# A bidirectional encoder trunk on one core: five seven-product pairs per feed-forward unit instead of three, with the residual added by transfers

## The chip, the cores and the metric

One Trainium2 chip, one of its cores. The metric is the device time of one execution in microseconds. The core has five engines, each of which takes its instructions in program order: PE (matrix multiply), DVE (elementwise, "VectorE"), ACT (activation functions, copies and casts, "ScalarE"), POOL (a general engine, "GpSimd") and SP, which here only starts transfers. Engines wait for one another by semaphores.

## The reference

A sequence of 256 tokens with 2048 features passes two layers. Each layer is `x = x + mixer(rmsnorm(x))`, then `x = x + swiglu(rmsnorm(x))`. The mixer of the first layer is grouped-query attention, that of the second a recurrent block. The change is in the feed-forward half of both layers:

```python
D_MODEL, SEQ, D_FF = 2048, 256, 5632

def rms_norm(x, g):
    y = x * lax.rsqrt(jnp.mean(x * x, axis=-1, keepdims=True) + EPS)
    return y * g

def swiglu(h, w_gate, w_up, w_down):
    return (jax.nn.silu(h @ w_gate) * (h @ w_up)) @ w_down

for i in range(DEPTH):              # DEPTH = 2
    h = rms_norm(x, norm_mix[i])
    ...                             # mixer
    x = x + swiglu(rms_norm(x, norm_ffn[i]), ffn_w_gate[i], ffn_w_up[i], ffn_w_down[i])
```

All data are float32.

## The kernel before

**Numbers in two parts.** PE multiplies in a reduced format. So each float32 operand is split into hi (the value cast, by ACT) and lo (the rest, value minus hi, by DVE), and a product of a 128 x 128 block of x with 512 columns of a weight is three matmuls: x hi by w hi, x lo by w hi, x hi by w lo (`product`, L294, L295, L297). Every weight passes once through the chain: a transfer into a `raw` tile, ACT's cast to `hi`, DVE's subtraction to `lo`, PE. There are five `raw` tiles, and in the feed-forward stage seven hi and seven lo tiles, used in turn; a tile is written again when its last reader is done.

**Units.** The 5632 hidden columns are 44 tiles of 128, taken four at a time in a *unit*: 11 units per layer, numbered 0 to 10. A unit computes 512 columns of gate and of up for all 256 tokens. It runs over eight *pairs* c0 to c7 of 128-row blocks of the 2048 rows. A plain pair is two `wide` calls, each with its own weight tile (1024 wide) and four products, eight products in all, into the banks c11 and c21, then c12 and c22. A *seven-product pair* uses Strassen's scheme in Winograd's form: seven products, from sums of the weight blocks made by DVE and sums of the x blocks made once per layer (`Norm.form`). Its products, in order, go to m1 (weight b11), c11 (b21), c12 (b22), p5 (t1), p7 (t3), p6 (t2) and c21 (t4). Its weights take three 1024-wide hi and lo tiles, called here A (b11 and b21), B (t1 and t3) and C (t2 and t4), and a half one, `ohi` and `olo` (b22). `load_seven` makes them: A's split, the sums t1 and t3, the split of b22, the sums t2 and t4, then the splits of B and C.

Behind the last seven-product pair of a unit ACT copies m1 out of its bank (L734), and DVE combines it with p6, p5 and p7 (L735 to L738). When c7 is done, DVE adds c11 and c21 (L741), ACT applies silu, DVE forms the hidden values (L744, L745) and transposes them in blocks of 32 (L377); 16 copies on ACT, the *turn* (L384), put the blocks in place, and ACT and DVE split the result (L747, L748).

**Down groups.** The units of a layer fall into five parts of 2, 2, 2, 2 and 3. From unit 3 on, each unit is preceded by two of the four groups that multiply the part before by its rows of w_down: a group is 512 output columns, 16 products for these parts, into two banks of the same pool as m1, p5, p7 and p6 (four banks, in turn). DVE adds a group's banks to the residual x (`add_residual`, L318). The last part's groups stand at the end of the layer and also feed the next norm.

**Order.** PE's order is that of the code; a scheduler sets that of the other engines when the program is built. `follow` ties casts to casts and rests to rests, so that weights are prepared in the order of use.

Tiles with the same tag share `bufs` buffers: a new one waits until the old one's readers are done.

Of the kernel before, what the change touches and what calls it, by code (L numbers as in the profile page):

```python
# [15 lines left out]
ALU = mybir.AluOpType  # L16
AX = mybir.AxisListType

P = 128
S = 256  # L20
D = 2048
KT = D // P
# [4 lines left out]
DFF = 5632  # L27
PARTS = [8, 8, 8, 8, 12]
UNIT = 4
SEVEN = (0, 3, 5)  # L30
FEWER = (0, 5)
FEW = (1, 2)
HALF = 8
CHUNK = HALF * P
WIDE = 512
RING = 5
MORE = 2
NW = D // WIDE
COMMON = {"nsq", "ssq", "nm", "nr", "rsq_s"}
EPS = 1e-6  # L40
LRU_C = 8.0
GRID_W = 64
# [31 lines left out]
def trunk(ctx, tc, w, out):  # L74
# [32 lines left out]
    ring, held, ft = [0], [], []  # L107
# [80 lines left out]
    def ffn_order(l):  # L188
        seq = []
        for what, i in ffn_plan():  # L190
            if what == "down":
                seq += pairs(w[f"w_down{l}_{i[0]}"][i[1]])
                continue
            both = [(w[f"w_gate{l}"][i, c], w[f"w_up{l}"][i, c]) for c in range(KT // 2)]
            seq += sum(([b] if c in (FEWER if i in FEW else SEVEN) else list(b) for c, b in enumerate(both)), [])
        return seq + out_order(w[f"w_down{l}_{len(PARTS) - 1}"], UNIT // 2)

    order = [w["w_k"][i] for i in range(2 * KT // 4)]
# [50 lines left out]
    def new_acc():  # L249
        return ps_a.tile([P, 2 * S], F32, tag="acc", name=nm("acc"))  # L250
# [41 lines left out]
    def product(o, x, wt, start, stop):  # L292
        (xh, xl), (wh, wl) = x, wt
        pe.matmul(o, xh, wh, start=start, stop=False)  # L294
        pe.matmul(o, xl, wh, start=False, stop=False)  # L295
        step()
        pe.matmul(o, xh, wl, start=False, stop=stop)  # L297
        step()

    def wide(accs, xs, k0, total, fresh=None):  # L300
        hi, lo = half()
        fresh = fresh or (k0 == 0, k0 == 0)
        for j in range(CHUNK // WIDE):
            k = k0 + j
            wh, wl = (t[:, j * WIDE : (j + 1) * WIDE] for t in (hi, lo))
            for a in range(2):
                product(accs[a], block(xs, k, a), (wh, wl), j == 0 and fresh[a], k == total - 1)

    def wide_project(xs, total, bank=new_acc):
# [62 lines left out]


    def turn_blocks(src, engines, own=None):
        turned = tmp("turned", (P, 2, WIDE), bufs=1)
        own = tmp("hid", (P, 2, WIDE), bufs=1) if own is None else own
        dve.transpose(turned, src)  # L377
        t = own.rearrange("p a (b c) -> p (a b) c", c=S)
        for i in range(4):
            of = turned[32 * i : 32 * i + 32].rearrange("p a (k j c) -> p k a j c", k=4, j=4)  # L380
            for j in range(4):
                to = t[32 * j : 32 * j + 32].rearrange("p k (a i c) -> p k a i c", a=2, i=4)
                eng = engines[(4 * i + j) % len(engines)]
                (eng.copy if eng is act else eng.tensor_copy)(to[:, :, :, i, :], of[:, :, :, j, :])  # L384
        return t

    class Norm:
# [14 lines left out]
            self.xs.append(t)  # L402

        def square(self, g, a):
            sq = tmp("nsq", (P, WIDE), bufs=1)
            o = x_tm[:, a, g * WIDE : (g + 1) * WIDE]
            return act.activation(sq, o, AF.Square, accum_out=self.ss[:, a, g : g + 1])

# [15 lines left out]
                    self.form(2 * g + i, t[:, 2 * i : 2 * i + 2, :])  # L424

        def form(self, c, src):
            v, t = (tmp(f"e{i}", (P, 2 * S), bufs=1).rearrange("p (a b) -> p a b", a=n) for i, n in ((0, 2), (1, 4)))
            for j in range(2):
                act.activation(v[:, j, :], src[:, j, :], AF.Copy, scale=col(self.g[0], self.g[1] + 2 * c + j))
            (a11, a21), (a12, a22) = ([v[:, j, a * P : (a + 1) * P] for a in range(2)] for j in range(2))  # L430
            for i, x, y, op in (
                (0, a21, a22, ALU.subtract), (1, a11, a21, ALU.subtract),
                (2, t[:, 0, :], a11, ALU.subtract), (3, a12, t[:, 2, :], ALU.add),
            ):
                pool.tensor_tensor(t[:, i, :], x, y, op)
# [275 lines left out]
    def ffn(norm, nxt):  # L711
        def bank():
            return ps_m.tile([P, 2 * S], F32, tag="pm", name=nm("pm"))

        def unit(seven):
            xs, r = norm.xs, [norm.r[:, a : a + 1] for a in range(2)]
            m1, p5, p7, p6 = (bank() for _ in range(4))
            c11, c21, c12, c22 = (new_acc() for _ in range(4))
            for c in range(KT // 2):
                if c not in seven:  # L720
                    wide((c11, c21), xs, 2 * c, KT, (False, False))
                    wide((c12, c22), xs, 2 * c, KT, (False, c == 1))
                    continue
                wt, first, end = half(), c == seven[0], c == seven[-1]
                n1, n3, n2, n4 = norm.forms[c]
                a11, a12, a22 = block(xs, 2 * c, 0), block(xs, 2 * c + 1, 0), block(xs, 2 * c + 1, 1)
                for o, x, y in (
                    (m1, a11, "b11"), (c11, a12, "b21"), (c12, n4, "b22"), (p5, n1, "t1"),
                    (p7, n3, "t3"), (p6, n2, "t2"), (c21, a22, "t4"),
                ):  # L730
                    product(o, x, wt[y], first, end and any(o is m for m in (m1, p5, p7, p6)))
                if end:
                    base, v, u, x = (tmp(f"e{i}", (P, 2 * S), bufs=1) for i in range(4))
                    act.copy(base, m1)  # L734
                    dve.tensor_tensor(u, base, p6, ALU.add)  # L735
# [3 lines left out]
            h = tmp("hid", (P, 2, 2 * S), bufs=1)  # L739
            for o, y, b in ((base, base, c11), (u, u, c21)):  # L740
                dve.tensor_tensor(o, y, b, ALU.add)  # L741
            for a, (o, y, b) in enumerate(((base, v, c12), (u, x, c22))):
                table_act(o, o, AF.Silu, scale=r[a])
                dve.tensor_tensor(h[:, a, :], b, y, ALU.subtract)  # L744
                dve.scalar_tensor_tensor(h[:, a, :], h[:, a, :], r[a], o, ALU.mult, ALU.mult)  # L745
            t, ht = act_four(), turn_blocks(h, (act,), h)
            act.copy(t[:, :, :S], ht)  # L747
            dve.tensor_tensor(t[:, :, S:], ht, t[:, :, :S].bitcast(F32), ALU.subtract)  # L748
            return [t[:, k, :] for k in range(UNIT)]

        hid = [[] for _ in PARTS]
        ends = np.cumsum(PARTS) // UNIT
        for what, i in ffn_plan():
            if what == "unit":
                hid[int(np.searchsorted(ends, i, "right"))] += unit(FEWER if i in FEW else SEVEN)
            else:
                add_residual(i[1], wide_project(hid[i[0]], PARTS[i[0]], bank), None)
        if nxt is not None:
            ln_exp_tables()
        groups(hid[-1], PARTS[-1], PARTS[-1] - UNIT, lambda: None, partial(add_residual, norm=nxt, store=nxt is None))  # L760
        scope.pop()
        ft.pop().close()
# [216 lines left out]
```

## Time and profile before

| | |
|---|---|
| median of three runs | 2001.21 us (2000.93 to 2001.96) |
| the profiled execution | 2001.05 us, span 1999.3 us |
| busy: PE, DVE, ACT, POOL | 99%, 82%, 65%, 13% of the span |
| granted PE clock | 0.999 |
| three loads that carry the FFN weights | 176 each, 512 KB, 3.6 to 4.4 us to landing |

A page gives busy time by engine, and by source line the groups of instructions with their idle time before them and what ended it. A timeline row reads: start in us, duration in us, engine, line, operation, output and inputs with partitions x elements, count, and in brackets the idle time before it with its releaser. A row of a waits view reads: waiting engine, line and tile, then the one waited for, total us, times, longest. A row of a stretch gives its length, then busy us and instruction count for PE, PE's weight loads, DVE, ACT and POOL, then the clock, the share of transfer engines busy and GB/s. Instructions of an engine overlap a little at their ends, so what a run of them costs is read from start to start.

### The profile page before, as it was taken

Reading aid. Unit: us, or ns where it says so; the run is one execution under the profiler, and the core shown is the slowest. Engines: PE = TensorE matmul, PEld = TensorE weight load, DVE = VectorE, ACT = ScalarE, POOL = GpSimd, SP = SyncE. Lnnn points to the kernel's source line nnn. Section 1 sums busy time; section 2 is a strip of 40 time slices with the busy share of each in tenths; the row PEclk is TensorE's granted clock in tenths of the full one; section 3 lists DMA queues with packets and bytes.
Section 4 is the critical chain, followed back from the end, with each engine's and each line's share of the span. In section 5 each row is a group of like instructions: output and inputs, shape, how many; then the busy total and the mean of one; then the engine's idle time right before and its main releaser. Section 6 shows DMA issues by size and latency. Waiting matters only on the chain.

```text
span 1999.3 us, 27804 instructions
## 1 busy us (share of the span) xinstructions
PE 1981.1 (99%) x9940; PEld 1686.6 (84%) x9940; DVE 1629.9 (82%) x2154; ACT 1297.6 (65%) x1995; POOL 256.4 (13%) x315
## 2 busy tenths in 40 slices
PE   9999999999999999999999999999999999999999
PEld 8888888888888888888899998878888888888887
DVE  7989688888788887886779886897878887888873
ACT  7556577666656666567688887867655666556662
POOL 0443140000000000000455450410000000000000
PEclk9999999999999999999999999999999999999999
DMA  8543646656565565656556555566566555655664
GB/s 308 164 127 127 201 153 210 226 189 191 189 232 193 187 200 199 223 189 199 193 180 196 178 170 185 175 208 202 185 215 213 187 192 187 231 200 181 198 206 132
DMA packets 108570, 386.05 MB, mean 193 GB/s; under 512 B 12176, under 2 KB 12432, under 8 KB 108304
## 3 DMA queue, kind: packets, MB, share of 16 engines
q1 hardware_dynamic: 108288, 384.26, 58.3%
q8 instruction: 78, 1.28, 0.3%
q14 instruction: 60, 0.49, 0.1%
q10 hardware_dynamic: 144, 0.02, 0.0%
HBM read 382.13 MB, written 2.10 MB: 192 GB/s over the span
## 4 chain that ended last, share of the span: by engine, by line
PE 87%; DVE 7%; POOL 2%; issue 1%; ACT 1%; DMA 1%; SPq 0%; DVEq 0%; ACTq 0%; POOLq 0%
PE acc L294 16%; PE acc L295 16%; PE acc L297 16%; PE pm L297 8%; PE pm L295 8%; PE pm L294 8%; PE acc L274 3%; PE acc L275 3%; PE acc L276 3%; DVE lo L129 2%; PE acc L263 1%; POOL hb L548 1%; PE pm L275 1%; PE pm L276 1%; PE pm L274 1%
## 5 line engine op out<-in xcount | busy, mean ns | idle before, releaser
L129 DVE TENSOR_TENSOR lo<-raw,hi 128x1024 fp32r<-128x1024 f32 (+1 forms) x581 | 712.0, 1242 | 170.2 <-ACT hi L128 167.0
L128 ACT CAST hi<-raw 128x1024 fp32r<-128x1024 f32 (+1 forms) x581 | 596.6, 1048 | 299.1 <-PE acc L295 227.5
L294 PE MATMUL acc<-hi,xg 128*128 128x512 f32 x1036 | 403.3, 389 | 1.8 <-DVE e L741 1.4
L297 PE MATMUL acc<-lo,xg 128*128 128x512 f32 x1036 | 403.0, 389 | 0.0
L295 PE MATMUL acc<-hi,xg 128*128 128x512 f32 x1036 | 403.0, 389 | 0.0
L146 ACT CAST hi<-ws 128x1024 fp32r<-128x1024 f32 x124 | 130.6, 1054 | 194.5 <-DVE ws L152 192.3
L294 PEld LDWEIGHTS acc<-hi,xg 128*128 128x128 f32 x1036 | 194.5, 188 | 43.2 <-DVE e L741 2.3
L297 PEld LDWEIGHTS acc<-lo,xg 128*128 128x128 f32 x1036 | 194.5, 188 | 40.3
L295 PEld LDWEIGHTS acc<-hi,xg 128*128 128x128 f32 x1036 | 194.5, 188 | 40.3
L294 PE MATMUL pm<-hi,act 128*128 128x512 f32 x512 | 199.2, 389 | 0.0
L295 PE MATMUL pm<-hi,act 128*128 128x512 f32 x512 | 199.2, 389 | 0.0
L297 PE MATMUL pm<-lo,act 128*128 128x512 f32 x512 | 199.2, 389 | 0.0
L384 ACT COPY hid<-turned 32x256 f32<-32x256 f32 x436 | 175.9, 404 | 23.9 <-DVE turned L377 14.7
L294 PE MATMUL acc<-hi,act 128*128 128x512 f32 x448 | 174.6, 390 | 0.0
L297 PE MATMUL acc<-lo,act 128*128 128x512 f32 x448 | 174.4, 389 | 0.0
L295 PE MATMUL acc<-hi,act 128*128 128x512 f32 x448 | 174.3, 389 | 0.0
L149 DVE TENSOR_TENSOR lo<-ws,hi 128x1024 fp32r<-128x1024 f32 x124 | 151.8, 1225 | 6.4 <-ACT hi L146 3.6
L384 POOL COPY hid<-turned 32x256 f32<-32x256 f32 x84 | 52.3, 623 | 797.5 <-DVE turned L377 706.1
L274 PE MATMUL acc<-xg,hi 128*128 128x256 f32 x512 | 144.8, 283 | 0.0
L275 PE MATMUL acc<-xg,hi 128*128 128x256 f32 x512 | 144.6, 282 | 0.0
L276 PE MATMUL acc<-xg,lo 128*128 128x256 f32 x512 | 144.4, 282 | 0.0
L263 PE MATMUL acc<-xg,hi 128*128 128x512 f32 x384 | 126.6, 401 | 1.9 <-DVE xg L399 1.9
(215 smaller groups left out, 3435.7 us busy)
## 6 DMA issues: line engine op xcount, KB each, us to landing
raw<-in_w_gate_dram SPq DMA_DIRECT2D x176, 512.0 KB, 4.3
raw<-in_w_up_dram SPq DMA_DIRECT2D x176, 512.0 KB, 3.6
raw<-in_w_down_dram SPq DMA_DIRECT2D x176, 512.0 KB, 4.4
raw<-in_w_in_dram SPq DMA_DIRECT2D x64, 512.0 KB, 4.4
raw<-in_w_qv_dram SPq DMA_DIRECT2D x40, 512.0 KB, 3.9
raw<-in_w_o_dram SPq DMA_DIRECT2D x32, 512.0 KB, 3.6
raw<-in_w_out_dram SPq DMA_DIRECT2D x32, 512.0 KB, 4.0
graw<-in_w_gates_dram SPq DMA_DIRECT2D x32, 256.0 KB, 4.1
```

Of the source, the lines that this page charges most:

```text
L128: behind("cast", act.copy(hi[:, sl], raw[:, sl]))
L129: behind("rest", dve.tensor_tensor(lo[:, sl], raw[:, sl], hi[:, sl].bitcast(F32), ALU.subtract))
L146: behind("cast", act.copy(hi, src))
L149: return lambda: behind("rest", dve.tensor_tensor(lo, src, hi[:].bitcast(F32), ALU.subtract))
L263: pe.matmul(acc, w, xs[k], start=(k == 0), stop=stop)
L274: pe.matmul(o, hi, x[:, :S], start=start, stop=False)
L275: pe.matmul(o, hi, x[:, S:], start=False, stop=False)
L276: pe.matmul(o, lo, x[:, :S], start=False, stop=stop)
L294: pe.matmul(o, xh, wh, start=start, stop=False)
L295: pe.matmul(o, xl, wh, start=False, stop=False)
L297: pe.matmul(o, xh, wl, start=False, stop=stop)
L384: (eng.copy if eng is act else eng.tensor_copy)(to[:, :, :, i, :], of[:, :, :, j, :])
```

## The change

Units 3 to 10 of both layers take seven-product pairs at c0, c1, c3, c4 and c5 in place of c0, c3 and c5. Unit 0 keeps c0, c3 and c5; units 1 and 2 have c1 and c5 in place of c0 and c5. Which matmul starts a bank is no longer fixed to the first pair but found by `fresh`.

A unit's scratch is two tiles, `one` (base and u, later the transposed blocks) and `two` (v and x, then the hidden values), in place of six. The norm's forms and squares share a two-buffer tag `form`.

The groups of the first four parts no longer end in DVE's add: ACT copies each bank into a `form` tile, and a transfer that POOL issues adds the tile to x.

```diff
-SEVEN = (0, 3, 5)
-FEWER = (0, 5)
-FEW = (1, 2)
+SEVEN = (0, 1, 3, 4, 5)
+FEWER = {0: (0, 3, 5), 1: (1, 5), 2: (1, 5)}
...
         def form(self, c, src):
-            v, t = (tmp(f"e{i}", (P, 2 * S), bufs=1).rearrange("p (a b) -> p a b", a=n) for i, n in ((0, 2), (1, 4)))
+            v, t = (tmp("form", (P, 2 * S)).rearrange("p (a b) -> p a b", a=n) for n in (2, 4))
...
+            def fresh(o):
+                n = len(new)
+                new[:] = [b for b in new if b is not o]
+                return len(new) < n
...
                 if end:
-                    base, v, u, x = (tmp(f"e{i}", (P, 2 * S), bufs=1) for i in range(4))
+                    one, h = (tmp(n, (P, 2, WIDE), bufs=1) for n in ("one", "two"))
+                    (base, u), (v, x) = ([t[:, a, :] for a in range(2)] for t in (one, h))
                     act.copy(base, m1)
...
             else:
-                add_residual(i[1], wide_project(hid[i[0]], PARTS[i[0]], bank), None)
+                for a, acc in enumerate(wide_project(hid[i[0]], PARTS[i[0]], bank)):
+                    t = tmp("form", (P, WIDE))
+                    act.copy(t, acc)
+                    pool.dma_start(out=x_tm[:, a, i[1] * WIDE : (i[1] + 1) * WIDE], in_=t, accum_op=ALU.add)
```

What the scheduler makes of it on ACT is shown at two places. Lines after the change are one lower than before up to `form`, and some seven higher from the unit on (L734 becomes L741).

The first place is c5 of a unit in the steady part of a layer. Before, ACT has A, the half tile, B and C of c5 (L146), then four plain casts (L128), then the copy of m1 (L734):

```order
L146 CAST hi_1528_7286<-raw_1524_7280 128x1024
L146 CAST ohi_1530_7292<-raw_1525_7281 128x512
L146 CAST hi_1532_7296<-ws_1526_7284 128x1024
L146 CAST hi_1534_7301<-ws_1527_7285 128x1024
L128 CAST hi_1541_7337<-raw_1540_7336 128x1024
L128 CAST hi_1544_7355<-raw_1543_7354 128x1024
L128 CAST hi_1547_7373<-raw_1546_7372 128x1024
L128 CAST hi_1550_7391<-raw_1549_7390 128x1024
L734 COPY e0_1536_7327<-pm_1474_7070 128x512
```

Now the copy is L741 and the casts of seven-product weights are L145, and at the same place stands:

```order
L145 CAST hi_1242_5825<-raw_1238_5819 128x1024
L145 CAST ohi_1244_5831<-raw_1239_5820 128x512
L741 COPY one_1250_5866<-pm_1176_5587 128x512
L145 CAST hi_1246_5835<-ws_1240_5823 128x1024
L145 CAST hi_1248_5840<-ws_1241_5824 128x1024
L127 CAST hi_1253_5874<-raw_1252_5873 128x1024
```

The copy of m1 has moved from four casts behind c5's last to ahead of c5's B and C (`hi<-ws`). It stands so in units 4 to 10 of both layers; in unit 3 it stands between B and C.

The second place is where a unit's epilogue meets the next unit's first pair. On ACT before, the turn (L384) and then all of c0's casts:

```order
L128 CAST hi_1581_7571<-raw_1580_7570 128x1024
L384 COPY hid_1552_7408<-turned_1554_7418 32x8x32 x16
L146 CAST hi_1595_7604<-raw_1591_7598 128x1024
L146 CAST ohi_1597_7610<-raw_1592_7599 128x512
L747 CAST act_1553_7417<-hid_1552_7408 128x4x256
L146 CAST hi_1599_7614<-ws_1593_7602 128x1024
L146 CAST hi_1601_7619<-ws_1594_7603 128x1024
```

Now the turn is L383, the split's cast L753 and the copies of a group's two banks L765:

```order
L145 CAST hi_1188_5601<-raw_1184_5595 128x1024
L145 CAST ohi_1190_5607<-raw_1185_5596 128x512
L765 COPY form_1158_5501<-pm_1144_5427 128x512
L765 COPY form_1159_5504<-pm_1145_5428 128x512
L145 CAST hi_1192_5611<-ws_1186_5599 128x1024
L383 COPY two_1129_5320<-one_1143_5407 32x8x32 x16
L145 CAST hi_1194_5616<-ws_1187_5600 128x1024
L145 CAST hi_1200_5648<-raw_1196_5642 128x1024
L145 CAST ohi_1202_5654<-raw_1197_5643 128x512
L753 CAST act_1142_5406<-two_1129_5320 128x4x256
L765 COPY form_1174_5581<-pm_1160_5507 128x512
L765 COPY form_1175_5584<-pm_1161_5508 128x512
```

The turn has moved from ahead of c0's A to between c0's B and C, behind the two copies of the first group's banks; the second group's copies stand ahead of c1's B and C. It is so in units 4 to 10 of both layers.

The third place is DVE's own order there. Before, the transpose (L377), a plain rest, the two residual adds of the first group, and only then c0 of the next unit:

```order
L377 STREAM_TRANSPOSE turned_1009_4818<-hid_1007_4808 128x1024
L129 TENSOR_TENSOR lo_1037_4972<-raw_1035_4970,hi_1036_4971 128x1024
L318 TENSOR_TENSOR x_75<-x_75,pm_1010_4838 128x512
L318 TENSOR_TENSOR x_75<-x_75,pm_1011_4839 128x512
L149 TENSOR_TENSOR lo_1051_5005<-raw_1046_4998,hi_1050_5004 128x1024
```

Now:

```order
L148 TENSOR_TENSOR olo_1191_5608<-raw_1185_5596,ohi_1190_5607 128x512
L376 STREAM_TRANSPOSE one_1143_5407<-two_1129_5320 128x1024
L151 TENSOR_TENSOR ws_1187_5600<-ws_1186_5599,raw_1185_5596 128x512
L151 TENSOR_TENSOR ws_1187_5600<-ws_1187_5600,raw_1184_5595 128x512
L148 TENSOR_TENSOR lo_1193_5612<-ws_1186_5599,hi_1192_5611 128x1024
L148 TENSOR_TENSOR lo_1195_5617<-ws_1187_5600,hi_1194_5616 128x1024
```

The transpose has moved into c0's work, ahead of t2 and t4, and the adds to x are gone.

More of the change, by code (lines that the diff above doesn't have):

```diff
@@ L38 @@
 NW = D // WIDE
-COMMON = {"nsq", "ssq", "nm", "nr", "rsq_s"}
+COMMON = {"ssq", "nm", "nr", "rsq_s"}
 EPS = 1e-6
@@ L194, in ffn_order @@
             both = [(w[f"w_gate{l}"][i, c], w[f"w_up{l}"][i, c]) for c in range(KT // 2)]
-            seq += sum(([b] if c in (FEWER if i in FEW else SEVEN) else list(b) for c, b in enumerate(both)), [])
+            seq += sum(([b] if c in (FEWER.get(i, SEVEN)) else list(b) for c, b in enumerate(both)), [])
         return seq + out_order(w[f"w_down{l}_{len(PARTS) - 1}"], UNIT // 2)
@@ L374, in turn_blocks @@
     def turn_blocks(src, engines, own=None):
-        turned = tmp("turned", (P, 2, WIDE), bufs=1)
-        own = tmp("hid", (P, 2, WIDE), bufs=1) if own is None else own
+        turned = tmp("one", (P, 2, WIDE), bufs=1)
+        own = tmp("two", (P, 2, WIDE), bufs=1) if own is None else own
         dve.transpose(turned, src)
@@ L404, in square @@
         def square(self, g, a):
-            sq = tmp("nsq", (P, WIDE), bufs=1)
+            sq = tmp("nsq" if not ft else "form", (P, WIDE), bufs=1 if not ft else 2)
             o = x_tm[:, a, g * WIDE : (g + 1) * WIDE]
@@ L718, in unit @@
             c11, c21, c12, c22 = (new_acc() for _ in range(4))
+            new = [m1, p5, p7, p6, c11, c21, c12, c22]
+            def fresh(o):
+                n = len(new)
+                new[:] = [b for b in new if b is not o]
+                return len(new) < n
             for c in range(KT // 2):
                 if c not in seven:
-                    wide((c11, c21), xs, 2 * c, KT, (False, False))
-                    wide((c12, c22), xs, 2 * c, KT, (False, c == 1))
+                    for pair in ((c11, c21), (c12, c22)):
+                        wide(pair, xs, 2 * c, KT, [fresh(o) for o in pair])
                     continue
-                wt, first, end = half(), c == seven[0], c == seven[-1]
+                wt, end = half(), c == seven[-1]
                 n1, n3, n2, n4 = norm.forms[c]
@@ L730, in unit @@
                 ):
-                    product(o, x, wt[y], first, end and any(o is m for m in (m1, p5, p7, p6)))
+                    product(o, x, wt[y], fresh(o), end and any(o is m for m in (m1, p5, p7, p6)))
                 if end:
-                    base, v, u, x = (tmp(f"e{i}", (P, 2 * S), bufs=1) for i in range(4))
+                    one, h = (tmp(n, (P, 2, WIDE), bufs=1) for n in ("one", "two"))
+                    (base, u), (v, x) = ([t[:, a, :] for a in range(2)] for t in (one, h))
                     act.copy(base, m1)
@@ L738, in unit @@
                     dve.tensor_tensor(x, u, p5, ALU.subtract)
-            h = tmp("hid", (P, 2, 2 * S), bufs=1)
             for o, y, b in ((base, base, c11), (u, u, c21)):
@@ L743, in unit @@
                 table_act(o, o, AF.Silu, scale=r[a])
-                dve.tensor_tensor(h[:, a, :], b, y, ALU.subtract)
-                dve.scalar_tensor_tensor(h[:, a, :], h[:, a, :], r[a], o, ALU.mult, ALU.mult)
+                dve.tensor_tensor(y, b, y, ALU.subtract)
+                dve.scalar_tensor_tensor(y, y, r[a], o, ALU.mult, ALU.mult)
             t, ht = act_four(), turn_blocks(h, (act,), h)
@@ L754, in ffn @@
             if what == "unit":
-                hid[int(np.searchsorted(ends, i, "right"))] += unit(FEWER if i in FEW else SEVEN)
+                hid[int(np.searchsorted(ends, i, "right"))] += unit(FEWER.get(i, SEVEN))
             else:
-                add_residual(i[1], wide_project(hid[i[0]], PARTS[i[0]], bank), None)
+                for a, acc in enumerate(wide_project(hid[i[0]], PARTS[i[0]], bank)):
+                    t = tmp("form", (P, WIDE))
+                    act.copy(t, acc)
+                    pool.dma_start(out=x_tm[:, a, i[1] * WIDE : (i[1] + 1) * WIDE], in_=t, accum_op=ALU.add)
         if nxt is not None:
```

## The prediction

> **What bounds the kernel now.** I read the page first, then a table by stretches, then who PE waits for, then the timelines of PE, ACT and DVE inside one feed-forward unit.
>
> ```profile
> span 1999.3 us, 27804 instructions
> PE 1981.1 (99%) x9940; PEld 1686.6 (84%) x9940; DVE 1629.9 (82%) x2154; ACT 1297.6 (65%) x1995; POOL 256.4 (13%) x315
> 404.40:467.60 63.20, 63.20 (x280) 52.34 (x280) 52.20 (x59) 38.36 (x51) 0.00 (x0) 1.00 0.61 200
> ```
>
> The third line is one unit and the two down groups beside it: 63.20 us, PE busy for all of it (second number), DVE for 52.20, ACT for 38.36, at full clock. Between 345 and 970 us PE waits for nobody; around the first units it waits three times:
>
> ```profile
> PE acc L294 <- DVE e L741: 1.4, 2, 1.1
> PE acc L294 <- ACT hi L128: 0.9, 1, 0.9
> PE acc L294 <- DVE x L318: 0.3, 1, 0.3
> ```
>
> So PE's matmuls are the time, and what they cost is read from where they start. These are matmuls of c5, the last seven-product pair of that unit:
>
> ```profile
> 453.19 0.39 PE L294 MATMUL pm<-hi,xg 128*128 128x512 f32 x1
> 453.64 0.39 PE L297 MATMUL pm<-lo,xg 128*128 128x512 f32 x1
> 455.23 0.39 PE L294 MATMUL pm<-hi,fh 128*128 128x512 f32 x1
> 455.68 0.39 PE L297 MATMUL pm<-lo,fh 128*128 128x512 f32 x1
> 456.14 0.39 PE L295 MATMUL pm<-hi,fl 128*128 128x512 f32 x1
> ```
>
> Product 1 (m1) starts at 453.19, product 4 (t1 into p5) at 455.23: three products in 2.04 us, 0.68 each. Each is three matmuls 0.227 apart; the third reads the lo tile and starts 0.45 after the first.
>
> **The gain.** Units 3 to 10 of both layers have five such pairs in place of three, each one product shorter: 2 x 8 x 2 = 32 products, 32 x 0.68 = 21.8 us of PE. A unit with its two groups goes from 93 products (63.24) to 91 (61.88), 1.36 less. Units 1 and 2 move a pair from c0 to c1; their products stay.
>
> **What it costs DVE and ACT.** The other rows of the unit:
>
> ```profile
> 420.82 1.22 DVE L748 TENSOR_TENSOR act<-hid,act 128x1024 fp32r<-128x1024 f32 x1
> 421.96 1.41 DVE L152 TENSOR_TENSOR ws<-ws,raw 128x512 f32<-128x512 f32 x2
> ...
> 431.43 1.22 DVE L149 TENSOR_TENSOR lo<-raw,hi 128x1024 fp32r<-128x1024 f32 x1
> 432.56 0.69 DVE L152 TENSOR_TENSOR ws<-raw,raw 128x512 f32<-128x512 f32 x1
> ...
> 434.37 1.41 DVE L152 TENSOR_TENSOR ws<-ws,raw 128x512 f32<-128x512 f32 x2
> 435.70 2.50 DVE L149 TENSOR_TENSOR lo<-ws,hi 128x1024 fp32r<-128x1024 f32 x2
> 438.12 2.35 DVE L129 TENSOR_TENSOR lo<-raw,hi 128x1024 fp32r<-128x1024 f32 x2
> ```
>
> Back to back, start to start, a seven-product pair takes DVE 438.12 - 431.43 = 6.69 us: A's lo 1.13, then t1, t3 and olo 434.37 - 432.56 = 1.81, t2 and t4 1.33, B's and C's lo 2.42. (A, B, C are its 1024-wide tiles: b11 and b21, t1 and t3, t2 and t4.) A plain pair takes 2 x 1.135 = 2.27; L748 takes 421.96 - 420.82 = 1.14. Two more such pairs add 8.84 to a unit; the four residual adds that leave give back 4 x 0.6. DVE goes from 52.2 to about 58.6 of 61.88 us: it still fits, if it need not wait. ACT gains three casts' worth of work (about 1 us each) and four 0.47 us copies, and stays near 70%. So the sum doesn't fall to throughput; it falls to two waits on ACT, which runs in order:
>
> ```profile
> 454.17 0.58 ACT L734 COPY e<-pm 128x512 f32<-128x512 f32 x1
> 454.64 1.05 ACT L128 CAST hi<-raw 128x1024 fp32r<-128x1024 f32 x1
> 456.56 1.05 ACT L128 CAST hi<-raw 128x1024 fp32r<-128x1024 f32 x1 [0.87 <-PE pm L295]
> 473.37 6.64 ACT L384 COPY hid<-turned 32x256 f32<-32x256 f32 x16 [0.74 <-DVE turned L377]
> 480.03 1.05 ACT L146 CAST hi<-raw 128x1024 fp32r<-128x1024 f32 x1
> 480.98 0.61 ACT L146 CAST ohi<-raw 128x512 fp32r<-128x512 f32 x1
> ```
>
> *Wait 1, the copy of m1.* Before, that copy (L734) stands behind all of c5's casts. In the new order it stands ahead of c5's B and C casts in units 4 to 10 of both layers (14 units), and between them in unit 3. It needs m1's last product, which is c5's own first one. From c5's start T: third matmul at T + 0.45, 0.39 long; 0.03 to the release (456.14 + 0.39 against 456.56); copy 454.64 - 454.17 = 0.47; cast of B 1.05; 0.03; lo of B 1.22; 0.03: T + 3.67. PE wants that lo at T + 455.68 - 453.19 = T + 2.49. At least 1.18 us of the 1.36 is lost there. In unit 3 only C is behind the copy; it is ready at about T + 3.7 and wanted 2 x 0.68 after B, at T + 3.85: nothing lost.
>
> *Wait 2, the turn.* Before, the 16 copies of the turn (6.64 us) stand ahead of the next unit's first cast, while DVE idles without harm. Now they stand between the next unit's c0 casts B and C, behind two copies that wait for PE's first down group. Let e be the end of that group's last matmul. ACT: second copy e + 0.03, cast of B e + 0.50, turn e + 1.46 (a cast's interval is 480.98 - 480.03 = 0.95), cast of C e + 8.12, done e + 9.17, so DVE resumes with C's lo at e + 9.2. Whether DVE's transpose is ready by then follows from these rows:
>
> ```profile
> 457.47 0.69 DVE L735 TENSOR_TENSOR e<-e,pm 128x512 f32<-128x512 f32 x1 [0.52 <-PE pm L297]
> 458.07 1.22 DVE L129 TENSOR_TENSOR lo<-raw,hi 128x1024 fp32r<-128x1024 f32 x1
> ...
> 469.64 1.40 DVE L745 SCALAR_TENSOR_TENSOR hid<-hid,nr,e 128x512 f32<-128x512 f32 x2
> 470.96 1.22 DVE L129 TENSOR_TENSOR lo<-raw,hi 128x1024 fp32r<-128x1024 f32 x1
> 472.10 1.24 DVE L377 STREAM_TRANSPOSE turned<-hid 128x1024 f32<-128x1024 f32 x1
> ```
>
> From the end of c5's lo of B, DVE has C 1.2, twelve plain tiles 12 x 1.135, eight epilogue adds of 0.60 and two of 0.66, then A, t1, t3 and olo of the next c0, 2.94, and the transpose, 1.24: 25.1 us. PE from the same lo has the rest of that product and three more, 2.3, two plain pairs and a group, 21.76, and 0.16: e is 24.2 behind it and the turn 25.7. So ACT's copies behind PE, not the transpose, set the turn. From e + 9.2 DVE has, without a pause until c5's B: 1.2 (C of c0), 6.69 (c1) + 1.14 (L748), 2.27 (c2), 13.38 (c3, c4), and 5.49 of c5, or 30.17: ready at e + 39.4. PE starts c5 after the second group (16 products, 10.88) and 36 products (24.48), less the 0.16 by which a matmul's end trails the next start: e + 35.2; it wants B's lo at e + 37.69. Stall 1.7 us in each of these 14 units; wait 1 lies inside it.
>
> **The other edits.** The 64 residual adds leave DVE and 64 copies and transfers come in. No row here shows a transfer from POOL that adds. Nearest rows:
>
> ```profile
> raw<-in_w_down_dram SPq DMA_DIRECT2D x176, 512.0 KB, 4.4
> x<-in_xt_dram SPq DMA_DIRECT2D x1, 2048.0 KB, 12.0
> ```
>
> One moves 256 KB, half of the first row, and has until the next group's copy needs its buffer, 10.88 us later. Even at 12.0 the copy would be 1 us late, and B of c1 behind it has some 2 us to spare: zero. Below zero it can't go, since no one but the last groups reads x. The five-pair forms add two per layer (ACT, POOL and DVE work while PE has the 21.8 us output groups; PE waits only 0.3 there): zero, up to 1 us a layer. Units 1 and 2 now begin on c11 and c21 instead of m1, so these must be free sooner (L741), but DVE does a plain pair there first and not a seven-product one, 4.4 us less. The 1.4 and 0.9 of PE waits quoted above may vanish or double: zero, between -2.3 and +2.3. The two scratch tiles are written and read in engine order; their reuse comes tens of us later: zero.
>
> **Sum.** -21.8 + 14 x 1.7 = +2.0, on the profiled execution's 2001.05 (span 1999.3), 0.16 below the median. I take 2003.
>
> **Rivals.** *The floor* (faster): DVE is quicker than my sum by half a us a unit, and only wait 1 is left: -21.8 + 14 x 1.18 = -5.3, 1996. For it: 30 us of DVE work is summed from single intervals. Against it: these intervals are from a stretch without idle time.
> *The full gain*: both waits are hidden, 1979. Against it: on ACT, B's cast can't pass the copy, and the copy can't pass c5's first product, so this would need shorter casts than any in the rows.
> *POOL and DVE collide* (slower). When POOL copies, DVE's adds of two SBUF tiles stretch in this trace:
>
> ```profile
> 265.00 7.96 POOL L384 COPY hid<-turned 32x256 f32<-32x256 f32 x8
> 265.94 0.88 DVE L152 TENSOR_TENSOR ws<-raw,raw 128x512 f32<-128x512 f32 x1
> 266.74 0.88 DVE L152 TENSOR_TENSOR ws<-raw 128x512 f32<-128x512 f32 x1
> ```
>
> An interval of 0.80 in place of 0.60. The second group's two transfers are issued where DVE has no slack. If POOL is at each for the length of one of its copies here (1.0 us), DVE loses 2 x 1.0 x 0.2/0.8 = 0.5 a unit, 14 x 0.5 = 7: 2010. It decides from 0.15 us a unit on. The Trainium skill, "SBUF — State Buffer", section "Who interferes with whom", says that a DVE instruction with two SBUF inputs is held up only by a GpSimd instruction that reads SBUF, and infers that descriptor writing needs the write side. The rows above agree as to reads; no run here shows the writing. By that rule this rival is worth 0 and the sum stays at 2003.
> *Late loads* (slower): c3's second raw tile is free when c1's t4 is done and has 5.8 us until its add; a load takes 4.4 in the row above. At 7 us, 14 x 1.2 = 17, 2020.
>
> **How the numbers follow.** A measurement of this kernel tells 0.2%, 4.0 us, from no change. My forecast 0.58 (its own range 1998 to 2008), floor 0.17, full gain 0.04, collision 0.16, late loads 0.05. Faster by more: the full gain and half of the floor, 0.13. Slower: collision, late loads and the part of the forecast above 2005.2 (a stall of 1.9 or more, about a third), 0.40. Same: the rest, 0.47. The range leaves out the full gain and late loads, and reaches from the floor to a little past the collision: 1996 to 2012.
>
> **What the changed profile would show.** If right: 96 fewer matmuls; PE waiting some 1.7 us, 14 times, for DVE's lo of t1 and t3 (L148) at c5; the m1 copy (L741) followed on ACT by two casts from ws; DVE idle 5 to 6 us once a unit for ACT's cast after the turn (L383); a unit period of 63.4 to 63.8 in place of 63.24. At the floor, PE's waits are 1.2 and DVE waits for ACT at c5. The collision shows as ws adds of 0.8 or more beside POOL. I am wrong outright if PE runs through c5 without a wait.

## The result, and the profile after

The changed kernel takes 2018.7 us (median of four runs, 2015.1 to 2019.3) against 2001.2 of the kernel before: ratio 1.0083, 95% interval 1.0071 to 1.0096. It is 17.5 us slower, and outside the predicted 1996 to 2012.

First the page of the changed kernel (span; busy time of the engines), then the seven units behind unit 3 with their down groups, from the first matmul of one group to that of another, and one such unit (length, then busy time of PE, PEld, DVE, ACT and POOL, granted clock, DMA share):

```profile
span 2016.8 us, 28134 instructions
PE 1974.7 (98%) x9844; PEld 1670.3 (83%) x9844; DVE 1716.7 (85%) x2286; ACT 1377.8 (68%) x2135; POOL 321.3 (16%) x395
471.45:917.13 445.68, 437.47 (x1912) 357.44 (x1911) 401.24 (x464) 301.40 (x407) 24.43 (x28) 1.00 0.69 215
535.07:598.71 63.64, 62.48 (x274) 51.08 (x273) 57.49 (x68) 42.95 (x59) 3.49 (x4) 1.00 0.70 216
```

The 96 matmuls are gone, and a unit takes 63.64 us where it took 63.24: DVE works 57.49 us in it and PE no longer runs through. What PE waits for (total, times, longest):

```profile
PE pm L296 <- DVE lo L148: 13.5, 15, 1.1
PE acc L293 <- DVE one L747: 9.0, 7, 2.1
PE pm L293 <- ACT hi L145: 3.5, 14, 0.3
```

The first (but for one of its 15 waits) and the third are the c5 of units 4 to 10, foretold; the second, the adds of c11 and c21, had been 1.4 us. One c5, on PE and on ACT:

```profile
583.12 0.40 PE L296 MATMUL acc<-olo,fh 128*128 128x512 f32 x1
583.77 0.51 PE L293 MATMUL pm<-hi,fh 128*128 128x512 f32 x1 [0.25 <-ACT hi L145]
584.11 0.39 PE L294 MATMUL pm<-hi,fl 128*128 128x512 f32 x1
585.41 0.50 PE L296 MATMUL pm<-lo,fh 128*128 128x512 f32 x1 [0.91 <-DVE lo L148]
582.18 0.59 ACT L741 COPY one<-pm 128x512 f32<-128x512 f32 x1 [2.02 <-PE pm L296]
582.67 1.05 ACT L145 CAST hi<-ws 128x1024 fp32r<-128x1024 f32 x1
```

From 583.12 to 585.41 PE starts three matmuls in 2.29 us where 0.68 is the undisturbed rate; with 0.11 behind them the stall is 1.7. ACT has stood idle 2.02 us at the copy of m1, and the cast of B comes behind it. Earlier in the unit, ACT's turn and what DVE waits for:

```profile
545.47 1.27 ACT L765 COPY form<-pm 128x512 f32<-128x512 f32 x2 [3.37 <-PE pm L296]
546.63 1.05 ACT L145 CAST hi<-ws 128x1024 fp32r<-128x1024 f32 x1
547.58 6.63 ACT L383 COPY two<-one 32x256 f32<-32x256 f32 x16
554.24 1.05 ACT L145 CAST hi<-ws 128x1024 fp32r<-128x1024 f32 x1
555.33 1.23 DVE L148 TENSOR_TENSOR lo<-ws,hi 128x1024 fp32r<-128x1024 f32 x1 [5.83 <-ACT hi L145]
```

ACT waits 3.37 us for PE at the copies of the group's banks, casts B, turns for 6.63 us and casts C; DVE idles 5.83 us until then. All of this stands in the prediction, and at the times it worked out from e, the end of the first group: with B's cast at e + 0.50 (546.63), C's cast was due at 554.25 and DVE at 555.3, c5 at 581.3 and B's lo at 585.5; the trace has 554.24, 555.33, 581.31 for c5's first matmul, and 585.41 for the matmul that reads that lo. What does not stand there is at the border between units 0 and 1, on PE, then on DVE, then the granted clock in two windows of 5 us (the number behind POOL's):

```profile
318.35 0.39 PE L296 MATMUL acc<-lo,xg 128*128 128x512 f32 x1
320.28 0.47 PE L293 MATMUL acc<-hi,xg 128*128 128x512 f32 x1 [1.54 <-DVE one L747]
320.82 0.40 PE L296 MATMUL acc<-lo,xg 128*128 128x512 f32 x1
323.12 0.80 PE L293 MATMUL acc<-hi,xg 128*128 128x512 f32 x1 [1.91 <-DVE one L747]
...
315.30 1.22 DVE L148 TENSOR_TENSOR lo<-raw,hi 128x1024 fp32r<-128x1024 f32 x1 [0.32 <-ACT hi L145]
319.45 0.68 DVE L747 TENSOR_TENSOR one<-one,acc 128x512 f32<-128x512 f32 x1
321.25 1.22 DVE L148 TENSOR_TENSOR lo<-ws,hi 128x1024 fp32r<-128x1024 f32 x1
322.38 0.68 DVE L747 TENSOR_TENSOR one<-one,acc 128x512 f32<-128x512 f32 x1
...
320.00:325.00 5.00, 2.82 (x8) 1.98 (x9) 5.00 (x8) 4.47 (x6) 0.00 (x0) 0.70 0.72 210
325.00:330.00 5.00, 5.00 (x16) 3.91 (x15) 5.00 (x6) 1.05 (x2) 0.00 (x0) 0.62 0.43 116
```

Unit 0's last matmul starts at 318.35. Unit 1's first product goes to c11 and waits until DVE has added the old c11 (319.45); the second goes to c21 and waits for that add (322.38). c21 had its last matmul four products, 2.7 us, before 318.35, and c11 one product earlier still, but DVE does A of unit 1's c1 (315.30), its sums and its B (321.25) in between. Then the clock falls, and PE runs at 16 matmuls in 5 us.

In the kernel before, DVE does both adds together, PE waits once, and the clock stays at 1.00 (PE, DVE, and the second window):

```profile
321.81 0.50 PE L294 MATMUL acc<-hi,xg 128*128 128x512 f32 x1 [1.13 <-DVE e L741]
321.07 1.28 DVE L741 TENSOR_TENSOR e<-e,acc 128x512 f32<-128x512 f32 x2
325.00:330.00 5.00, 5.00 (x24) 4.14 (x23) 5.00 (x6) 3.08 (x4) 0.00 (x0) 1.00 0.76 228
```

Where the 17.5 us lie is read from one matmul after another that both timelines have (start in us):

| the matmul | before | after | difference |
|---|---|---|---|
| in the attention part | 183.76 | 182.23 | -1.5 |
| first of the groups behind unit 2, layer 0 | 405.59 | 409.57 | +4.0 |
| the same, behind unit 3 | 468.83 | 471.45 | +2.6 |
| first of the last groups, layer 0 | 911.51 | 917.13 | +5.6 |
| first of the recurrence's output groups | 1209.58 | 1219.01 | +9.4 |
| groups behind unit 2, layer 1 | 1424.18 | 1438.07 | +13.9 |
| groups behind unit 3, layer 1 | 1487.42 | 1499.97 | +12.6 |
| first of the last groups, layer 1 | 1930.10 | 1945.72 | +15.6 |
| end of the span | 1999.3 | 2016.8 | +17.5 |

Units 3 to 10 of both layers (unit 3, then the seven others, layer by layer): -1.36 + 3.00 - 1.34 + 3.07 = +3.4. The first stretch of each feed-forward part, with the border: +5.5 and +4.5. Between the last groups and the recurrence's end +3.8, the end +1.9, the start -1.5.

### The profile page after: what moved, and what is told of

It is laid out like the page before. It is cut to its first block, busy times and chain, and to the rows that moved or that the text cites. A ratio compares the mean times of both kernels' runs of the same rounds, so it can differ in the third digit from the quotient of the medians.

```text
span 2016.8 us, 28134 instructions
## 1 busy us (share of the span) xinstructions
PE 1974.7 (98%) x9844; PEld 1670.3 (83%) x9844; DVE 1716.7 (85%) x2286; ACT 1377.8 (68%) x2135; POOL 321.3 (16%) x395
## 4 chain that ended last, share of the span: by engine, by line
PE 62%; DVE 22%; ACT 7%; issue 7%; POOL 1%; DMA 0%; DVEq 0%; ACTq 0%; SPq 0%; POOLq 0%
PE acc L293 11%; PE acc L296 11%; PE acc L294 11%; DVE ws L151 6%; DVE lo L148 5%; PE pm L296 5%; PE pm L294 5%; PE pm L293 5%; ACT two L383 4%; DVE lo L128 3%; PE acc L273 3%; PE acc L274 3%; ACT hi L145 3%; PE acc L275 3%; DVE olo L148 2%
## 5 line engine op out<-in xcount | busy, mean ns | idle before, releaser
L128 DVE TENSOR_TENSOR lo<-raw,hi 128x1024 fp32r<-128x1024 f32 (+1 forms) x517 | 634.7, 1247 | 115.3 <-ACT hi L127 112.1
L127 ACT CAST hi<-raw 128x1024 fp32r<-128x1024 f32 (+1 forms) x517 | 528.4, 1047 | 202.8 <-PE acc L294 95.3
L293 PE MATMUL acc<-hi,xg 128*128 128x512 f32 x844 | 330.6, 392 | 7.4 <-DVE one L747 7.4
L294 PE MATMUL acc<-hi,xg 128*128 128x512 f32 x844 | 330.1, 391 | 0.0
L296 PE MATMUL acc<-lo,xg 128*128 128x512 f32 x844 | 329.8, 391 | 0.0
L145 ACT CAST hi<-ws 128x1024 fp32r<-128x1024 f32 x188 | 197.7, 1052 | 182.1 <-DVE ws L151 145.1
L148 DVE TENSOR_TENSOR lo<-ws,hi 128x1024 fp32r<-128x1024 f32 x188 | 229.8, 1224 | 89.1 <-ACT hi L145 85.6
L766 POOL DMA_DIRECT2D x<-form x64 | 56.0, 999 | 1116.3 <-ACT form L765 1116.2
L293 PEld LDWEIGHTS acc<-hi,xg 128*128 128x128 f32 x844 | 159.4, 189 | 42.0 <-DVE one L747 4.7
L294 PEld LDWEIGHTS acc<-hi,xg 128*128 128x128 f32 x844 | 159.6, 189 | 33.3
L383 ACT COPY two<-one 32x256 f32<-32x256 f32 x436 | 176.0, 404 | 9.4 <-DVE one L376 3.7
L151 DVE TENSOR_TENSOR ws<-ws,raw 128x512 f32<-128x512 f32 x188 | 129.6, 689 | 3.0
```

Source lines behind the costliest of these rows:

```text
L127: behind("cast", act.copy(hi[:, sl], raw[:, sl]))
L128: behind("rest", dve.tensor_tensor(lo[:, sl], raw[:, sl], hi[:, sl].bitcast(F32), ALU.subtract))
L145: behind("cast", act.copy(hi, src))
L148: return lambda: behind("rest", dve.tensor_tensor(lo, src, hi[:].bitcast(F32), ALU.subtract))
L151: behind("rest", dve.tensor_tensor(o, x, y, ALU.add))
```

## The experiments

Theory A is the prediction's two waits for units 4 to 10, and the order of DVE at the border for the rest. Ratios are against the kernel before, timed alongside.

**start_back**: units 1 and 2 as before.

```diff
-FEWER = {0: (0, 3, 5), 1: (1, 5), 2: (1, 5)}
+FEWER = {0: (0, 3, 5), 1: (0, 5), 2: (0, 5)}
```

> Units 1 and 2 have their seven-product pairs at c0 and c5 again; everything else is as in the changed kernel. Theory A: of the 17.5 us by which the changed kernel is slower, about 10 come from the border between units 0 and 1 of each layer (+5.5 and +4.5 us in the two traces), where unit 1 now begins on banks c11 and c21 before DVE has added unit 0's, and PE's clock then drops. By it this kernel takes 2009 us (2007 to 2011), and the first down group starts within 1.5 us of where it did before. Rival: the border only shows a clock that would have dropped anyhow, and DVE's added work near unit 3 sets it: 2016 or more.

2009.5 us, ratio 1.004 (1.0026 to 1.0054): 9 us of the 17.5 hang on this one line. The groups behind unit 2 start at 404.49. From the matmul in the attention part (182.36) that is 222.1 us, against 221.8 in the kernel before and 227.3 in the changed kernel. PE's waits for L747 fall from 9.0 us to

```profile
PE acc L293 <- DVE one L747: 3.6, 6, 0.9
```

**copy_last**: the m1 copy behind c5's casts.

```diff
-                    act.copy(base, m1)
+                    follow(act.copy(base, m1), newest["cast"])
```

> The copy of m1 is ordered behind c5's last cast, as it stood in the kernel before; nothing else changes. Theory A (the prediction's): in units 4 to 10 the wait that decides is the turn between c0's casts, which leaves DVE 1.7 us late at c5, and the m1 copy lies inside it. By it the stall per unit stays 1.6 to 1.8 us and the time within 2 us of the changed kernel's 2018.7. Rival: the m1 copy is what delays c5's B, and DVE would be in time without it: 14 units give back up to 1.7 us each, 1995 us. Between them, if DVE is late by less than the copy costs: 14 x 0.5 = 7 us, 2012.

2016.8 us, ratio 1.0079 (1.0064 to 1.0095), a unit still at 63.69:

```profile
535.59:599.28 63.69, 62.44 (x275) 51.09 (x273) 57.34 (x67) 43.00 (x58) 3.49 (x4) 1.00 0.68 213
```

So the copy of m1, which the changed kernel's trace shows ahead of B's cast with 2 us of idle time, costs nothing by itself: DVE's lo of B is late anyhow.

**turn_split**: half of the turn on POOL.

```diff
-            t, ht = act_four(), turn_blocks(h, (act,), h)
+            t, ht = act_four(), turn_blocks(h, (act, pool), h)
```

> Every second of the 16 turn copies goes to POOL, so ACT has 8 of them (3.3 us in place of 6.6). The order on ACT moves with it: in the units looked at, the turn stands ahead of c0's cast of B, and the m1 copy behind all of c5's casts. Theory A: both waits of the prediction go, units 4 to 10 take 61.9 to 62.2 us in place of 63.6, and the time falls by 14 x 1.4 to 1.7 = 20 to 24 us, to 1995 to 1999; the border at unit 1 and the clock drops remain. Rival (collision): POOL's 8 copies of about 1.0 us stretch DVE's adds of two SBUF tiles from 0.6 to 0.8 us, DVE has no slack left, and the units stay at 62.8 or more: 2007 or more.

1991.3 us, ratio 0.9951 (0.9938 to 0.9965): 27 us less than the changed kernel, more than the 20 to 24 expected. The seven units behind unit 3 give 12.5 us of it in layer 0 and 12.6 in layer 1; the rest is for the most part PE's waits for L747 behind unit 10 (under "Not counted at all" below), which go too. PE runs through the units, at the length of its 91 products:

```profile
533.49:595.37 61.88, 61.88 (x275) 51.27 (x273) 59.14 (x67) 39.98 (x50) 10.20 (x12) 1.00 0.69 221
539.83 7.08 POOL L383 COPY two<-one 32x256 f32<-32x256 f32 x8 [43.73 <-DVE one L376]
541.22 0.88 DVE L151 TENSOR_TENSOR ws<-raw,raw 128x512 f32<-128x512 f32 x1
542.02 0.88 DVE L151 TENSOR_TENSOR ws<-raw 128x512 f32<-128x512 f32 x1
540.42 3.31 ACT L383 COPY two<-one 32x256 f32<-32x256 f32 x8
```

The turn itself is no shorter, for POOL's eight copies take 7.08 us where ACT's sixteen took 6.63. What is freed is ACT, after 3.31. The collision is there (sums of 0.88 beside POOL's copies, starting 0.80 apart), and DVE's work grows from 57.5 to 59.1 us a unit; with 61.88 to do it in, that costs nothing. The order on ACT moved with the split, so this run alone doesn't part length from place.

**turn_early**: the place alone, in units 4 to 10; all 16 copies stay on ACT.

```diff
         first = two(sums[0], ("t1", "t3"))
+        if "turn" in newest:
+            follow(newest["cast"], newest.pop("turn"))
 ...
```

> In units 4 to 10 the turn's 16 copies, all on ACT, are ordered ahead of c0's cast of B, where the kernel before has them (there even ahead of c0's first cast). Theory A: it is the unbroken 6.6 us on ACT that holds DVE up, not the place: the turn then ends 7.6 us behind the first group's end, B's cast 8.7, and DVE still has B and C to do where in the changed kernel only C was left; it is 0.6 us later at c5, so 14 x 0.6 = 8 us slower than the changed kernel, 2027 (2020 to 2032). Rival: the place between the casts is the fault, and with the old place the waits go: 2000 or less.

2018.3 us, ratio 1.0089 (1.0075 to 1.0103). The rival is out: ahead of B's cast, the place that turn_split has, 16 copies on ACT bring nothing, so there it is the length that counts. (Ahead of c0's first cast, as in the kernel before, was not tried with five pairs.) The expectation missed too: it had 2020 to 2032, and this kernel can't be told from the changed one. The seven units of layer 0 take 448.84 us in place of 445.68 (3.2 more, 4.2 expected), those of layer 1 only 0.5 more, and stalls alternate between units, since the scheduler also moved the copy of m1 in some.

**transfers_alone**: three pairs a unit and the old start, with the transfers and the two scratch tiles.

```diff
-SEVEN = (0, 1, 3, 4, 5)
-FEWER = {0: (0, 3, 5), 1: (1, 5), 2: (1, 5)}
+SEVEN = (0, 3, 5)
+FEWER = {0: (0, 3, 5), 1: (0, 5), 2: (0, 5)}
```

> Of the change only the residual transfers and the two scratch tiles are in: seven-product pairs c0, c3, c5 in the later units and c0, c5 in units 1 and 2, as before. Theory A: the transfers cost PE nothing, since DVE has 11 us of slack a unit and the buffers are free 10.9 us before they are wanted: 2001 us, within 2. Rival: transfers and weight loads share the DMA engines (the loads take 0.1 to 0.3 us longer in the changed kernel), or the copies on ACT hold up casts: 0.3 us or more a unit over 16 units, 2006 or more.

2000.7 us, ratio 0.9998 (0.9989 to 1.0007). A unit takes what it took, and DVE has 2.4 us less to do (49.78 against 52.20). The last line is the transfers (count, size, us to landing):

```profile
528.44:591.68 63.24, 63.24 (x280) 52.42 (x279) 49.78 (x55) 40.24 (x54) 3.46 (x4) 1.00 0.70 217
x<-form POOLq DMA_DIRECT2D x64, 256.0 KB, 6.4
```

**pairs_alone**: five pairs, residual adds on DVE.

```diff
-                for a, acc in enumerate(wide_project(hid[i[0]], PARTS[i[0]], bank)):
-                    ...
+                add_residual(i[1], wide_project(hid[i[0]], PARTS[i[0]], bank), None)
```

> Five pairs per unit, but the residual adds are on DVE as before, with no copies on ACT and no transfers. Theory A: DVE then has 61.0 us of work a unit, and the wait for ACT's turn is still there (its copies stand between c0's casts of B and C; no copy that waits for PE is ahead of them, so it ends about 0.6 us sooner, and DVE's two adds of the second group cost 1.2): stall 2.3 in place of 1.7, 14 x 0.55 = 8 us more than the changed kernel, 2026 (2022 to 2034). Rival: the copies on ACT that wait for PE's group are what makes the turn late, and without them the turn is in time: 2005 or less.

2026.8 us, ratio 1.0132 (1.0115 to 1.0149), 8 more than with the transfers. The same seven units:

```profile
471.17:920.92 449.75, 440.72 (x1913) 356.52 (x1911) 417.13 (x491) 287.02 (x379) 0.00 (x0) 1.00 0.57 197
```

So the copies that wait for PE are not what makes the turn late; the transfers are worth 8 us beside the five pairs, and nothing beside three.

**adds_first**: DVE adds c11 and c21 before the next unit's first A.

```diff
-                dve.tensor_tensor(o, y, b, ALU.add)
+                newest["adds"] = dve.tensor_tensor(o, y, b, ALU.add)
 ...
         two(raw[0], ("b11", "b21"))()
+        if "adds" in newest:
+            follow(newest["rest"], newest.pop("adds"))
```

> DVE's lo of the first A tile of a unit is ordered behind the unit before's adds of c11 and c21. At the border between units 0 and 1 this puts both adds ahead of unit 1's A, its sums and its B, where the changed kernel has them between and behind these. Theory A: that order is why PE waits 1.9 and 2.3 us there (c21's add ends 322.98, though its last product was done about 316), and the waits let the clock drop: both waits and the drop go, 5 to 6.5 us in each layer, and the time falls to 2006 to 2009, with units 1 and 2 still beginning on c11 and c21. Rival: DVE is short of time at the border whatever its order, because two pairs of unit 1 lie closer together than before; the wait moves to A or B of unit 1's c1, and the time stays above 2014.

2004.6 us, ratio 1.0021 (1.0011 to 1.003): 14 us less than the changed kernel, with units 1 and 2 still on (1, 5). Both adds now stand at 316.08, ahead of A:

```profile
316.08 1.28 DVE L749 TENSOR_TENSOR one<-one,acc 128x512 f32<-128x512 f32 x2
317.28 1.22 DVE L148 TENSOR_TENSOR lo<-raw,hi 128x1024 fp32r<-128x1024 f32 x1
```

From the matmul in the attention part to the groups behind unit 2 the time is now 0.6 us less than in the kernel before, and 0.2 less in the same stretch of layer 1. So with DVE's amount of work and the start on a plain pair as they were, the order alone takes the border's cost away; start_back shows that the start alone does so too. It took both, a start on c11 and c21 and their late adds. The time is below the expected 2006 to 2009: of the 14 us, the groups behind unit 2 start 6.4 sooner in layer 0, and layer 1's first stretch is 4.7 shorter; 1.3 lie between the layers and 1.8 in layer 1's units, which the expectation did not count.

**fill_border**: PE kept busy while it waits (`fill` is (7, 9) at unit 1's c0).

```diff
             for a in range(2):
+                for _ in range(fill[a] if fill and j == 0 else 0):
+                    pe.matmul(spare[0], block(xs, k, a)[0], wh, start=True, stop=True)
                 product(accs[a], ...)
 ...
```

> PE does 7 extra matmuls ahead of unit 1's first product and 9 ahead of its second, into the bank of m1, which the real product overwrites later; they take 1.6 and 2.0 us, inside the two waits of 1.7 to 2.2 and 2.1 us. Nothing else changes. Theory A: the half-rate stretch behind these waits (about 12 matmuls 0.43 apart in layer 0, 8 in layer 1, 2.4 and 1.6 us) is the clock's answer to an idle PE, so with PE busy it goes and the waits stay: the time falls by 4 us, to 2014.5 (2013 to 2016). Rival: the half rate has another cause (loads or DVE's writes at that moment), and stays: 2018 to 2019, or later by what the extra matmuls add.

2013.1 us, ratio 1.0066 (1.0051 to 1.0081): 5.6 less than the changed kernel, for 32 matmuls more. The clock is 1.00 in the windows at both borders, two of which were at 0.70 and 0.62:

```profile
320.00:325.00 5.00, 5.00 (x23) 3.70 (x21) 5.00 (x9) 4.46 (x5) 0.00 (x0) 1.00 0.48 129
325.00:330.00 5.00, 5.00 (x23) 4.16 (x23) 5.00 (x6) 3.04 (x5) 0.00 (x0) 1.00 0.31 103
```

The first stretch of layer 0 is 2.75 us shorter than in the changed kernel and that of layer 1 2.05, 4.8 together: so much of the border's 10 us is the clock and not the waiting. This is one trace, but its four times (2011.5 to 2014.2) all lie below the changed kernel's, and of the twelve borders with such waits in six traces without filling (the changed kernel, copy_last, turn_split, turn_early, pairs_alone, fill_gates) eleven show the drop.

**fill_gates**: the same at the recurrence's start.

```diff
     def three(o, hi, lo, x, start, stop, spare=None, n=(0, 0)):
+        fill(spare, n[0])
         pe.matmul(o, hi, x[:, :S], start=start, stop=False)
+        fill(spare, n[1])
 ...
```

> At the start of the recurrence, where the first gate product waits three times for its input (losses of 1.3, 0.65 and 1.0 us in the changed kernel), PE does 6, 3 and 5 extra matmuls of 0.19 us on a constant into a spare bank. Theory A: the stretch at half rate behind these waits (granted clock 0.81, then 0.51 in two 5 us windows at 1005 to 1015; about 2.7 us lost) is the clock's answer to an idle PE; it goes, and the time falls by 2 to 3 us against the changed kernel, to 2016. In runs where the clock doesn't drop there anyhow, nothing is gained. Rival: the half rate is not from PE being idle and stays: 2018.7.

2016.2 us, ratio 1.008 (1.0066 to 1.0094). The median is where theory A had it, but the interval overlaps the changed kernel's (1.0071 to 1.0096). The clock there, of the changed kernel and then of this one:

```profile
1005.00:1010.00 5.00, 2.61 (x14) 2.03 (x14) 4.90 (x10) 2.13 (x3) 1.53 (x3) 0.81 0.82 253
1010.00:1015.00 5.00, 5.00 (x26) 5.00 (x25) 2.02 (x5) 2.90 (x6) 2.14 (x4) 0.51 0.64 224
...
1005.00:1010.00 5.00, 4.08 (x37) 3.92 (x36) 5.00 (x10) 1.98 (x3) 2.22 (x5) 1.00 0.81 256
1010.00:1015.00 5.00, 5.00 (x45) 5.00 (x44) 4.08 (x8) 3.40 (x7) 2.37 (x5) 1.00 0.71 243
```

The drop is gone, and from the last groups of layer 0 to the recurrence's output groups the time is 1.4 us shorter, not 2.7. That the filling did it is not shown: start_back keeps a clock of 1.00 at this place without it. And in the same trace layer 1's border kept its clock without any filling, so the median would not be this edit's alone.

**best_new_start**: turn_split and adds_first together.

> Both repairs at once: every second turn copy on POOL, and the adds of c11 and c21 ahead of the next unit's A. Theory A: they act at different places and add up: 1991.3 from the split turn, less 10 to 12 us of the two borders: 1980 (1978 to 1983). Rival: the border's 2 us waits were partly hidden behind late loads (ACT waits 1.6 and 1.1 us for transfers there), and only the clock part comes back: 1986 or more.

1980.2 us, ratio 0.9903 (0.9888 to 0.9918): faster than both kernels. The page and one unit:

```profile
span 1978.1 us, 28240 instructions
PE 1960.6 (99%) x9844; PEld 1668.9 (84%) x9844; DVE 1747.4 (88%) x2286; ACT 1310.3 (66%) x1959; POOL 474.5 (24%) x571
529.39:591.27 61.88, 61.88 (x274) 51.24 (x273) 59.13 (x67) 39.97 (x50) 10.20 (x12) 1.00 0.69 221
```

That is 19.5 us below the kernel before timed alongside (1999.7), and the prediction's gain was 21.8: the products were worth nearly what they were counted at, and the long turn on ACT and the order on DVE had taken it.

## Why the prediction was wrong, point by point

- *The gain, 1.36 a unit*: right. Unit 3, without a wait, moves the difference by -1.36 and -1.34, and both repaired kernels have units of 61.88.
- *Wait 2 decides at 1.7 us, wait 1 inside it*: right. Forecast unit period 63.4 to 63.8, measured 63.64; copy_last shows the second half. Seven units took 445.68 - 7 x 61.88 = 12.5 us over, 1.8 each. Units 3 to 10 come to +3.4 where the sum had +2.0.
- *Late loads, 2020*: this rival fell, and that the measured time lies near its price is chance. The three loads of FFN weights landed in 4.6, 3.9 and 4.5 us, not 7, and DVE's sums waited for none of them. ACT did wait 55.1 us for loads of w_down (0.4 before), but turn_split has 37.3 us of that and PE runs through its units.
- *Transfers and scratch at zero*: right (transfers_alone), though a transfer landed in 4.6 us in the changed kernel and 6.4 in transfers_alone where 4.4 was the nearest row.
- *The POOL and DVE collision*: the rival fell as far as the transfers go. DVE's sums ws<-ws,raw have a median of 0.688 us in the changed kernel and 0.691 before. Here a sum and a rest, each of two SBUF tiles, beside an issue of two transfers at 558.48 that took POOL 1.75 us:

```profile
558.21 0.68 DVE L151 TENSOR_TENSOR ws<-raw 128x512 f32<-128x512 f32 x1
558.81 0.69 DVE L148 TENSOR_TENSOR olo<-raw,ohi 128x512 fp32r<-128x512 f32 x1
```

  By the Trainium skill, "SBUF — State Buffer", section "Who interferes with whom", only a GpSimd instruction that reads SBUF holds such an add up; the trace now agrees on both sides, 0.68 beside an issue and 0.88 beside POOL's copies (turn_split).
- *"Units 1 and 2 now begin on c11 and c21 ... zero, between -2.3 and +2.3"*: this term failed. The stretches with this border measured +5.5 and +4.5 us, 10 of the nearly 16 by which the forecast was short. It was argued from how much work DVE has before the border ("a plain pair there first, 4.4 us less"); what decides is the place of two adds among that work. c21 had been the bank of unit 1's seventh product and became that of its second; its add stood behind the next pair's A, sums and B. adds_first moves these two adds and takes the border's cost away, with the work and the start as they were. And the range counted waits alone: the clock's drop behind them (fill_border: 4.8 us for both borders) had no term.
- *Not counted at all*: unit 10's same two adds are late for the last groups, whose first accumulators use these banks, by 1.2 us in layer 0 and 1.4 in layer 1 (the longest wait of layer 0 is shown). They go with the long turn: turn_split has no wait for these adds there.

```profile
918.77 0.50 PE L293 MATMUL acc<-hi,act 128*128 128x512 f32 x1 [0.70 <-DVE one L747]
```

  Nor was the clock at the recurrence's start counted: start_back, with waits there of 1.00, 0.41 and 0.85 us (here 1.13, 0.41 and 0.85) and a clock of 1.00, is 2.7 us quicker between the last groups of layer 0 and the recurrence's output groups. That this is owed to the change is not shown: the kernel before has start_back's waits there and keeps its clock, transfers_alone has them with three pairs a unit and does not (0.81, then 0.85). The last 0.9 us at the end and the -1.5 at the start (there the profile of the kernel before has a low clock of its own, 0.87 in the first 10 us) were not followed up.

## What to carry to other kernels

When a change gives a unit another first accumulator, look up, in the order and not in the load, where the engine that must free that accumulator does so: two adds of 0.6 us in the wrong place cost 10 us here, the clock included. A long unbroken run of small copies on an in-order engine (6.6 us) delayed whoever needed the next cast even though that engine was a third idle; splitting it over a second engine was worth 27 us. Where PE waits some 2.4 to 4 us in sum, close together, leave room in the range for the clock: here it mostly fell behind such waits, and cost 2.75 and 2.05 us at the two borders and 2.7 at the recurrence.

## What the runs showed of the hardware

PE's clock fell to half after two waits of 1.5 and 1.9 us with only three matmuls between them (changed kernel, layer 0); behind start_back's border, whose one wait is 0.85, it stayed at 1.00. It doesn't always fall: in fill_gates the border has waits of 0.96 and 1.92 us in layer 0, with the clock at 0.71 behind them, and 1.06 and 1.91 in layer 1, with 1.00:

```profile
325.00:330.00 5.00, 5.00 (x17) 3.97 (x16) 5.00 (x7) 1.94 (x3) 0.00 (x0) 0.71 0.36 121
1350.00:1355.00 5.00, 5.00 (x22) 4.14 (x23) 5.00 (x6) 3.02 (x5) 0.00 (x0) 1.00 0.38 112
```

Matmuls at half rate, 0.427 apart in place of 0.227, stand from 323.12 to 328.83 in layer 0 of the changed kernel, 5.7 us, and for 3.5 in layer 1. The Trainium skill, "TensorE: Matmul & The Clock Gate", section "What's actually happening", says that the clock goes to half after at least one idle window of about 3.4 us, comes back after about 3.4 us of work, and that the window runs freely, whatever the kernel does. The trace agrees with the free-running window (like waits, once with a drop and once without) and with the least length of the drop. But no single wait here was as long as 3.4 us, and PE did three matmuls between the two, so in these traces a mostly idle PE was enough.
